# Where VectorE reads a plain key, multiplies by the cosine and forms weight sums in an attention layer

## The chip, the cores and the metric

The kernel runs on one core of one Trainium2 chip. A core has five engines that run at the same time, each through its own queue in order: TensorE (PE, matrix products; PEld is its weight load), VectorE (DVE), ScalarE (ACT), GpSimd (POOL) and SyncE (SP), whose queue issues the DMA loads here. They wait for each other through semaphores. PE, DVE and ACT reach the accumulators in PSUM; everything else lies in SBUF.

The metric is the device time of one execution in microseconds (us), the median over repeated runs. A profile is one further execution, recorded instruction by instruction; its span runs from the first to the last instruction of the program.

## The reference

The model is a trunk of two layers on one sequence of 512 positions and width 1024, in float32: a dilated attention mixer, a gated ConvFFN, a Mamba-2 mixer, another ConvFFN, a final norm. The change lies in the attention mixer alone. There are 8 heads of width 128 and three groups of queries, keys and values, with dilations 1, 4 and 16:

```
qkv = (h @ w_qkv).reshape(bsz, s, N_ATTN_GROUPS, 3, ATTN_HEADS_PER_GROUP, ATTN_HEAD_DIM)
q = apply_partial_rope(qkv[:, :, :, 0], cos, sin)
k = apply_partial_rope(qkv[:, :, :, 1], cos, sin)
...
o_g, lse_g = dilated_window_attention(q[:, :, g], k[:, :, g], v[:, :, g], dil, ATTN_WINDOWS[g] // dil)
```

`apply_partial_rope` turns the first 32 of a head's 128 rows: each is multiplied by a cosine, and its partner row, multiplied by a sine, is added. The results of the three groups are mixed by a softmax over their log sums, and a product with `w_o` and the residual follow.

## The kernel before

Weights come as float32 and are split into a high and a low part (`hi` by ACT, `lo` by a DVE subtraction of two SBUF operands, L127 and L128, or L328 and L331); each block of a product is three PE matmuls (`mm3`, L138). The normalised input lies in SBUF, split in the same way (`xh`, `xl`).

A head needs seven projections: a query and a key in each of three groups, and the value `v0` of group 0 (groups 1 and 2 have theirs from a separate step). They are made in two ways:

- Plain: `ready` loads and splits the weights, `qk_products` makes 24 matmuls into a PSUM bank, and `qk_read` (L460) reads it: DVE multiplies by the cosine table `cr` out of PSUM (L464), DVE swaps the 32 rows with their partners (`stream_shuffle`, L467), POOL multiplies them by the sine table (L468) and adds them to the tile (L469). Group 0 is always plain.
- As a `Pair` (L475), query and key of group 1 or 2 together, with seven products of half size in place of eight: `load_sevens` (L302) issues four loads; `sums()` forms four sums of weights on DVE, each of 512 columns (L317, L318, L320, L321; L318 reads what L317 wrote, L320 what L318 wrote); `split("ab")`, `split("cd")` split the four weights; `block(i)` makes 12 matmuls; `query` and `key` add the products up out of PSUM on DVE and end in a shuffle and POOL's sine product (`swap`, L537); `turn` (L543) makes the cosine multiplication on DVE (L546) and the sum of the 32 rows on POOL (L547).

`v0_step` makes the product of `v0`; DVE scales it into the tile `tv` (L554); `v0_turn` has PE transpose it (L561, tile `pv`).

`attend(h)` is a generator with the steps of one head's attention: scores of four blocks of 128 queries (`scores(0)`, `scores(2)`: PE L659 to L661, then DVE masks and takes maxima, L665 and L669), exponentials on ACT, the shares of the groups (`join`), transposes of the probabilities (L714), products with the values (L722, L727), and the head's output `o` (ACT L759, DVE L760). The scores of a head read its plain key after L469.

`attend_and_project(h)` (L813) runs head h's attention between the projections of head m = h + 1, for h = 0 to 5. It holds two pairs: `one`, group 1 of head m, loaded and split by the head before, and `two`, group 2, loaded and split here. After them come the plain query and key of group 0 and `v0`. `next_pair(m + 1)` (L572), the generator `follow`, prepares the next head's `one`: its first step makes the pair's loads and its four sums, the second splits a and b, the third c and d. (For the last head, whose projections are all plain, it loads two plain weights in place of that.) For h = 3 the steps in `after` stand in its place. Before the first head, L591 to L634 do the same for head 0, and `following` prepares head 1.

Order: inside `tc.manual_schedule(engines=WRITTEN)` PE, DVE and ACT take their instructions in the order in which the program text makes them. POOL and SP are ordered by a planner that simulates the program. Buffers come from small rings: four of 1024 columns for raw weights, two for the fourth raw weight, two for the shuffled rows; a load waits until the user of its buffer is done.

Of the kernel before, what the change touches and what calls it, by code (L numbers as in the profile page):

```python
# [53 lines left out]
def trunk(ctx: ExitStack, tc: tile.TileContext, A, out):  # L54
# [23 lines left out]
    def t2(name, tag, bufs, pool=k2, dtype=F32):  # L78
        return pool.tile([P, 512], dtype, tag=tag, name=name, bufs=bufs)
# [69 lines left out]
    def project(src, name, low=V, cut=None):  # L149

        if name in early:
            return early.pop(name)
        if name in begun:
            t, hi, lo, at = begun.pop(name)
        else:
            hi, lo = loaded.pop(name) if name in loaded else load_unit(src, name, low=low)
            t, at = mm_bank(name), 0
        for k in range(at, KD):
            if cut and cut[0] == k:
                cut[1]()  # L160
            mm3(t, hi, lo, k, xh[k], xl[k], k == 0, k == KD - 1)
        return t
# [233 lines left out]
    def combine(j):  # L396

        x1, x2 = xps[2 * j], xps[2 * j + 1]
        w1, w2, m1 = col(C_MIX + 2 * j), col(C_MIX + 2 * j + 1), minus[:, 2 * j : 2 * j + 1]
        (ah, al), (bh, bl) = high_low(f"ta{j}"), high_low(f"tb{j}")  # L400
        d, t = (t2(f"{n}{j}", "pr", 7, s3) for n in ("d", "t"))
        e, t4 = d[:, H1], d[:, H0]
        V.tensor_tensor(d[:, H0], x1[:, H1], x1[:, H0], op=ALU.subtract)
        SC.activation(e, x2[:, H1], AF.Copy, scale=w2)
        SC.activation(ah[:, H0], d[:, H0], AF.Copy, scale=w1)
        V.scalar_tensor_tensor(
            al[:, H0], d[:, H0], w1, ah[:, H0].bitcast(F32), op0=ALU.mult, op1=ALU.subtract
        )
        V.scalar_tensor_tensor(t[:, H0], d[:, H0], m1, e, op0=ALU.mult, op1=ALU.add)
        V.scalar_tensor_tensor(t[:, H1], x1[:, H1], m1, e, op0=ALU.mult, op1=ALU.add)  # L410
        V.scalar_tensor_tensor(t4, x2[:, H0], w2, t[:, H0], op0=ALU.mult, op1=ALU.subtract)
        for h, l, at, src in ((ah, al, H1, t[:, H0]), (bh, bl, H0, t[:, H1]), (bh, bl, H1, t4)):
            SC.copy(h[:, at], src)
            V.tensor_tensor(l[:, at], src, h[:, at].bitcast(F32), op=ALU.subtract)
        combined.append(((ah, al), (bh, bl)))
# [31 lines left out]
    def name_of(h, g, c):  # L447
        return f"qk{h}{g}{c}"

    def ready(h, g, c):  # L450
        u = A["wqk"][h * 7 + 2 * g + c]
        loaded[name_of(h, g, c)] = load_unit(u, name_of(h, g, c))

    def ready_v0(h):
        loaded[f"v0{h}"] = load_unit(A["wqk"][h * 7 + 6], f"v0{h}")

    def qk_products(h, g, c, cut=None):
        return project(A["wqk"][h * 7 + 2 * g + c], name_of(h, g, c), cut=cut)

    def qk_read(h, g, c, p):  # L460
        n = name_of(h, g, c)
        t = t2(n, "qk", 10, s3)
        at, of = (in_blocks, by_residue) if g == 0 else ((lambda ap: ap),) * 2
        V.tensor_tensor(at(t), of(p), of(cr), op=ALU.mult)  # L464
        rot = t2("rot" + n, "rot", 2, s3)
        R = slice(0, ROPE)
        V.stream_shuffle(rot[R, :], p[R, :], SWAP)  # L467
        G.tensor_tensor(rot[R, :], rot[R, :], sr[R, :], op=ALU.mult)  # L468
        G.tensor_tensor(at(t)[R], at(t)[R], of(rot)[R], op=ALU.add)  # L469
        qk[h, g, c] = t  # L470
# [4 lines left out]
    class Pair:  # L475
# [53 lines left out]
        def key(self):  # L529
            k = self.out[1]  # L530
            V.tensor_tensor(k[:, H0], self.s[0], self.r[2], op=ALU.add)
            V.tensor_tensor(k[:, H1], k[:, H0], self.s[1], op=ALU.add)
            V.tensor_tensor(k[:, H0], k[:, H0], self.r[3], op=ALU.add)
            self.swap(1)
            self.turn(1)

        def swap(self, c):  # L537
            R = slice(0, ROPE)
# [11 lines left out]
    def v0_step(h):  # L550
        n = f"v0{h}"
        p = project(A["wqk"][h * 7 + 6], n)
        t = t2("t" + n, "vt", 1, s3)
        V.tensor_tensor(in_blocks(t), by_residue(p), by_residue(rbc), op=ALU.mult)  # L554
        v0[h] = t

    def v0_turn(h):
        t = v0[h]
        pv = aux_bank("pv")
        for j in range(4):  # L560
            T.transpose(pv[:, j * P : (j + 1) * P], t[:, j * P : (j + 1) * P], ident)  # L561
        v0[h] = t2(f"v0{h}", "v0", 2, s3)
        SC.copy(v0[h], pv)
# [8 lines left out]
    def next_pair(h):  # L572

        if h == NH - 1:
            ready(h, 0, 0)
            yield
            ready(h, 0, 1)
            yield
        else:
            pair = begun_pair[h] = Pair(h, 1)  # L580
            pair.sums()
            yield
            pair.split("ab")
            yield
            pair.split("cd")
        yield
# [4 lines left out]
    with tc.manual_schedule(engines=WRITTEN):  # L591
        load2(1)
        V.tensor_tensor(cr, cr, rbc, op=ALU.mult)
        second[0]()
        combine(1)
        load2(2)
        V.tensor_tensor(sr[0:ROPE, :], sr[0:ROPE, :], rbc[0:ROPE, :], op=ALU.mult)
        second[1]()
        combine(2)
        load2(3)  # L600
        second[2]()
        combine(3)
        ready(0, 0, 0)
        one = Pair(0, 1)
        second[3]()
        one.sums()
        one.split("ab")
        p = qk_products(0, 0, 0)
        qk_read(0, 0, 0, p)
        one.split("cd")  # L610
        ready(0, 2, 0)
        for i in range(3):
            one.block(i)
        one.query(0)
        for i in range(3, 6):
            one.block(i)
        one.query(1)
        ready(0, 2, 1)
        one.block(6)
        one.turn(0)  # L620
        one.key()
        p = qk_products(0, 2, 0)
        ready(0, 0, 1)
        qk_read(0, 2, 0, p)
        p = qk_products(0, 2, 1)
        ready_v0(0)
        qk_read(0, 2, 1, p)
        p = qk_products(0, 0, 1)
        qk_read(0, 0, 1, p)
        following = next_pair(1)  # L630
        next(following)
        next(following)
        v0_step(0)
        next(following)  # L634
# [178 lines left out]
    def attend_and_project(h, after=()):  # L813

        core, m = attend(h), h + 1
        follow = next_pair(m + 1)
        with tc.manual_schedule(engines=WRITTEN):
            one, two = begun_pair.pop(m), Pair(m, 2)
            next(core)
            next(core)  # L820
            v0_turn(h)
            two.sums()
            one.block(0)
            one.block(1)
            two.split("a")
            one.block(2)
            one.query(0)
            two.split("b")
            for i in range(3, 6):
                one.block(i)  # L830
            one.query(1)
            one.block(6)
            one.turn(0)
            one.key()
            next(core)
            two.split("c")
            two.block(0)
            two.block(1)
            next(core)
            two.block(2)  # L840
            two.query(0)
            two.split("d")
            ready(m, 0, 0)
            for i in range(3, 6):
                two.block(i)
            two.query(1)
            ready(m, 0, 1)
            next(core)
            two.turn(0)
            next(core)  # L850
            next(core)
            two.block(6)
            two.key()
            p = qk_products(m, 0, 0)
            qk_read(m, 0, 0, p)
            ready_v0(m)
            if not after:
                next(follow)
            p = qk_products(m, 0, 1, cut=(6, lambda: next(core)))
            next(core)  # L860
            qk_read(m, 0, 1, p)
            for f in after[:2] or (lambda: next(follow),) * 2:
                f()
            v0_step(m)
            next(core, None)
            for f in after[2:]:
                f()
# [950 lines left out]
```

## Time and profile before

| | |
|---|---|
| median of three runs | 1627.27 us (1624.9 to 1629.9) |
| the profiled execution | 1625.19 us |
| its span | 1623.4 us |
| mean granted TensorE clock | 0.996 |
| PE busy | 1599.6 us, 99% of the span |
| DVE, ACT, POOL busy | 1247.5, 787.7 and 579.7 us |

A row of the timeline gives start and duration in us, engine, line, operation, the tile written and those read, shape and count, and in brackets the time for which the engine was idle before it and what ended that. Consecutive instructions with the same tiles are one row, and rows overlap a little, because an engine starts an instruction before the one ahead has drained. A row of the waits gives the total, the number and the longest. A row of the windows gives a stretch, its length, each engine's busy time (and instructions), the granted clock of TensorE, and the DMA load. Attention with its projections takes the span's first 490 us.

### The profile page before, as it was taken

The page shows a single profiled execution, that of the slowest core. Times are in us where ns is not written, and L with a number is a line of the kernel's source. Part 1 is how long each engine was busy: PE and PEld are TensorE (multiplying, and loading weights), DVE is VectorE, ACT ScalarE, POOL GpSimd, SP SyncE. Part 2 cuts the span into 40 slices and gives each one's busy share as a digit, 9 for nine tenths or more (in the row PEclk, how much of TensorE's full clock was granted, in tenths as well). Part 3 has the DMA queues.
Part 4 walks back from the last instruction along what each step waited for, and adds up shares of the span by engine and source line. Part 5 has one row for each costly group of instructions (what it writes and reads, how often), then busy time and mean ns, then how long its engine had stood idle before and what let it go on. Part 6 is the DMA issues. An engine that isn't in the chain of part 4 may idle for free.

```text
span 1623.4 us, 24013 instructions
## 1 busy us (share of the span) xinstructions
PE 1599.6 (99%) x9080; PEld 1408.0 (87%) x9080; DVE 1247.5 (77%) x1949; ACT 787.7 (49%) x1362; POOL 579.7 (36%) x432
## 2 busy tenths in 40 slices
PE   9999999999999999999999999999999999999998
PEld 8888889898888889989988888888888888988987
DVE  7798887388556778868857889988898687876864
ACT  5355455265564544444445455544453454444443
POOL 0434444044432554653321222220122275365230
PEclk9999999999999999999999999999999999999999
DMA  6322223223334323423423333243332322342341
GB/s 220 92 85 88 82 72 111 72 79 98 98 117 148 112 66 97 151 60 96 140 82 119 120 118 115 92 127 127 127 115 78 101 84 76 102 133 79 93 129 52
DMA packets 63331, 168.48 MB, mean 104 GB/s; under 512 B 7344, under 2 KB 10800, under 8 KB 63216
## 3 DMA queue, kind: packets, MB, share of 16 engines
q1 hardware_dynamic: 62656, 166.42, 32.6%
q8 instruction: 71, 1.16, 0.3%
q10 hardware_dynamic: 560, 0.53, 0.1%
q14 instruction: 44, 0.36, 0.1%
HBM read 163.19 MB, written 3.74 MB: 103 GB/s over the span
## 4 chain that ended last, share of the span: by engine, by line
PE 87%; DVE 7%; ACT 3%; POOL 2%; issue 1%; DVEq 0%; POOLq 0%; ACTq 0%
PE u L136 29%; PE v L136 6%; PE z L136 5%; PE wso L136 5%; PE xs L136 5%; PE qk L136 5%; PE b L136 3%; PE c L136 3%; PE wo L136 2%; PE wd L136 2%; PE wz L136 2%; POOL rotqk L468 1%; ACT oth L686 1%; ACT pr L707 1%; PE py L1391 1%
## 5 line engine op out<-in xcount | busy, mean ns | idle before, releaser
L136 PE MATMUL u<-xh,hi_u 128*128 128x512 f32 x704 | 269.4, 383 | 0.0
L136 PE MATMUL u<-xh,lo_u 128*128 128x512 f32 x704 | 269.0, 382 | 0.0
L136 PE MATMUL u<-xl,hi_u 128*128 128x512 f32 x704 | 266.6, 379 | 0.0
L128 DVE TENSOR_TENSOR lo_u<-raw_u,hi_u 128x1024 fp32r<-128x1024 f32 x88 | 123.8, 1416 | 39.8 <-ACT hi_u L127 39.8
L136 PEld LDWEIGHTS u<-xh,lo_u 128*128 128x128 f32 x704 | 131.7, 187 | 24.5
L136 PEld LDWEIGHTS u<-xl,hi_u 128*128 128x128 f32 x704 | 131.7, 187 | 23.9
L136 PEld LDWEIGHTS u<-xh,hi_u 128*128 128x128 f32 x704 | 131.7, 187 | 22.2 <-issue 0.4
L127 ACT CAST hi_u<-raw_u 128x1024 fp32r<-128x1024 f32 x88 | 91.8, 1048 | 106.7 <-PE u L136 61.3
L960 DVE SCALAR_TENSOR_TENSOR au<-u,par,au 128x511 f32<-128x511 f32 (+1 forms) x152 | 113.4, 746 | 20.4 <-ACT au L958 18.0
L541 POOL TENSOR_TENSOR rotqk<-rotqk,sr 32x512 f32<-32x512 f32 x26 | 53.2, 2047 | 184.6 <-DVE rotqk L540 184.6
L985 POOL TENSOR_TENSOR au<-au,au 128x512 f32<-128x512 f32 x43 | 58.0, 1348 | 169.0 <-DVE au L960 155.2
L1336 POOL TENSOR_TENSOR xdd<-xdt,dec 128x384 f32<-128x384 f32 x16 | 18.0, 1139 | 240.3 <-DVE xdt L1335 240.3
L973 DVE TENSOR_TENSOR u<-u,rbc 128x512 f32<-128x512 f32 x76 | 52.9, 696 | 63.8 <-PE u L136 63.4
L468 POOL TENSOR_TENSOR rotqk<-rotqk,sr 32x512 f32<-32x512 f32 x22 | 51.2, 2327 | 71.2 <-DVE rotqk L467 71.2
L958 ACT ACTIVATE au<-u,par 128x512 f32<-128x512 f32 x76 | 59.1, 778 | 24.1 <-DVE u L973 22.5
L136 PE MATMUL qk<-xh,hi_qk 128*128 128x512 f32 x176 | 68.3, 388 | 0.0
L136 PE MATMUL qk<-xh,lo_qk 128*128 128x512 f32 x176 | 67.5, 384 | 0.0
L136 PE MATMUL qk<-xl,hi_qk 128*128 128x512 f32 x176 | 66.9, 380 | 0.0
L1136 POOL TENSOR_TENSOR xr<-xr,sums 128x512 f32<-128x512 f32 x16 | 33.1, 2067 | 82.6 <-DVE sums L1134 82.6
L239 POOL TENSOR_TENSOR ssum<-ssum,sq 128x512 f32<-128x512 f32 x21 | 32.5, 1547 | 83.7 <-ACT sq L238 83.3
L1445 POOL TENSOR_TENSOR lm<-lm,cb 128x512 f32<-128x512 f32 x32 | 47.5, 1508 | 25.5 <-ACT lm L1378 25.5
L982 ACT ACTIVATE au<-au 128x512 f32<-128x512 f32 x44 | 27.8, 631 | 54.9 <-DVE au L960 54.9
(3988 smaller groups left out, 5089.7 us busy)
## 6 DMA issues: line engine op xcount, KB each, us to landing
raw_u<-in_wup SPq DMA_DIRECT2D x88, 512.0 KB, 3.5
raw_qk<-in_wqk SPq DMA_DIRECT2D x22, 512.0 KB, 3.4
raw_xs<-in_win SPq DMA_DIRECT2D x16, 512.0 KB, 3.8
raw_z<-in_win SPq DMA_DIRECT2D x16, 512.0 KB, 3.5
lm<-rows SPq DMA_DIRECT2D x32, 256.0 KB, 5.3
raw_wso<-in_wso SPq DMA_DIRECT2D x16, 512.0 KB, 3.4
raw_v<-in_wv SPq DMA_DIRECT2D x12, 512.0 KB, 4.1
raw_wd<-in_wdn SPq DMA_DIRECT2D x16, 384.0 KB, 3.3
```

The lines of the kernel that those rows point to most:

```text
L127: SC.copy(hi[:, s], raw[:, s])
L128: low.tensor_tensor(lo[:, s], raw[:, s], hi.bitcast(F32)[:, s], op=ALU.subtract)
L136: T.matmul(in_turns(dst), w, in_turns(x), start=first, stop=last, skip_group_check=skip)
L239: add.tensor_tensor(ssum, ssum, sq, op=ALU.add)
L468: G.tensor_tensor(rot[R, :], rot[R, :], sr[R, :], op=ALU.mult)
L541: G.tensor_tensor(rot[R, :], rot[R, :], sr[R, :], op=ALU.mult)
L958: latest["tap"] = SC.activation(dst, src, AF.Identity, bias=col(c_b), scale=col(c_w + taps - 1))
L960: V.scalar_tensor_tensor(dst[:, j:], src[:, : S - j], col(c_w + taps - 1 - j), dst[:, j:], op0=ALU.mult, op1=ALU.add,)
L973: V.tensor_tensor(dst, p, rbc, op=ALU.mult)
L985: by.tensor_tensor(ab[1], ab[0], ab[1], op=ALU.mult)
L1136: G.tensor_tensor(low3, low3, v.unsqueeze(1).to_broadcast([P, 2, 256]), op=ALU.add)
L1445: G.tensor_tensor(t, t, cb, op=ALU.mult)
```

## The change

Three parts, all in the order in which the text makes instructions; no computation is added or removed.

- `key()` no longer ends in `turn(1)`; each of its three callers calls it. Two call it straight behind `key()`. In `attend_and_project` the `turn(1)` of `one` stands behind the second scores' masks and maxima and behind `two.split("c")`.
- In `attend_and_project` with no `after`, the first step of `follow` (the next pair's loads and sums) stands behind the read of the plain key of group 0 and no longer ahead of its product.
- Before the first head, the first step of `following` stands ahead of the product of head 0's plain key, no longer behind its read.

```
@@ class Pair, key()
             V.tensor_tensor(k[:, H0], k[:, H0], self.r[3], op=ALU.add)
             self.swap(1)
-            self.turn(1)
@@ before the first head
         one.turn(0)
         one.key()
+        one.turn(1)
         p = qk_products(0, 2, 0)
...
         qk_read(0, 2, 1, p)
+        following = next_pair(1)
+        next(following)
         p = qk_products(0, 0, 1)
         qk_read(0, 0, 1, p)
-        following = next_pair(1)
-        next(following)
         next(following)
         v0_step(0)
         next(following)
@@ attend_and_project
             one.key()
             next(core)
             two.split("c")
+            one.turn(1)
             two.block(0)
...
             two.block(6)
             two.key()
+            two.turn(1)
             p = qk_products(m, 0, 0)
             qk_read(m, 0, 0, p)
             ready_v0(m)
-            if not after:
-                next(follow)
             p = qk_products(m, 0, 1, cut=(6, lambda: next(core)))
             next(core)
             qk_read(m, 0, 1, p)
-            for f in after[:2] or (lambda: next(follow),) * 2:
+            for f in after[:2] or (lambda: next(follow),) * 3:
                 f()
             v0_step(m)
```

More of the change, by code (lines that the diff above doesn't have):

```diff
@@ L534, in key @@
             self.swap(1)
-            self.turn(1)
         def swap(self, c):
@@ L621, in trunk @@
         one.key()
+        one.turn(1)
         p = qk_products(0, 2, 0)
@@ L627, in trunk @@
         qk_read(0, 2, 1, p)
+        following = next_pair(1)
+        next(following)
         p = qk_products(0, 0, 1)
         qk_read(0, 0, 1, p)
-        following = next_pair(1)
-        next(following)
         next(following)
@@ L836, in attend_and_project @@
             two.split("c")
+            one.turn(1)
             two.block(0)
@@ L853, in attend_and_project @@
             two.key()
+            two.turn(1)
             p = qk_products(m, 0, 0)
@@ L856, in attend_and_project @@
             ready_v0(m)
-            if not after:
-                next(follow)
             p = qk_products(m, 0, 1, cut=(6, lambda: next(core)))
@@ L861, in attend_and_project @@
             qk_read(m, 0, 1, p)
-            for f in after[:2] or (lambda: next(follow),) * 2:
+            for f in after[:2] or (lambda: next(follow),) * 3:
                 f()
```

## The prediction

> **What bounds the kernel now.** I read the page first, then PE's waits from 50 to 480 us, then the timelines of PE, DVE and POOL around the longest of them, then the windows for the clock.
>
> ```profile
> span 1623.4 us, 24013 instructions
> PE 1599.6 (99%) x9080; PEld 1408.0 (87%) x9080; DVE 1247.5 (77%) x1949; ACT 787.7 (49%) x1362; POOL 579.7 (36%) x432
> ```
>
> ```profile
> PE sc L659 <- POOL qk L469: 11.8, 4, 3.0
> PE pv L561 <- DVE tv L554: 2.1, 1, 2.1
> PE qk42r L136 <- DVE loc_qk L331: 0.4, 1, 0.4
> ...
> PE qk52r L136 <- DVE loc_qk L331: 0.3, 1, 0.3
> ```
>
> PE sets the end; what the change can save is PE's idle time and what follows from it. Scores waited four times, some 3 us each, for the plain key that POOL finishes late. Once the transposes of `v0` waited for DVE, and in six heads one weight product waited 0.35 us for a split. The page itself counts 24 us without a busy PE. Here is the first long wait, on POOL, DVE and PE.
>
> ```profile
> 122.00 1.26 POOL L547 TENSOR_TENSOR qk<-qk,rotqk 32x512 f32<-32x512 f32 x1
> 123.23 2.24 POOL L468 TENSOR_TENSOR rotqk<-rotqk,sr 32x512 f32<-32x512 f32 x1
> 125.55 1.61 POOL L469 TENSOR_TENSOR qk<-qk,rotqk 32x512 f32<-32x512 f32 x1
> 130.38 4.43 POOL L468 TENSOR_TENSOR rotqk<-rotqk,sr 32x512 f32<-32x512 f32 x1 [3.22 <-DVE rotqk L467]
> 134.89 1.60 POOL L469 TENSOR_TENSOR qk<-qk,rotqk 32x512 f32<-32x512 f32 x1
> ```
>
> ```profile
> 122.13 2.22 DVE L128 TENSOR_TENSOR lo_v<-raw_v,hi_v 128x1024 fp32r<-128x1024 f32 x1
> 124.27 1.75 DVE L317 TENSOR_TENSOR rawa_qk<-q_qk,rawb_qk 128x512 f32<-128x512 f32 x1
> 126.06 1.66 DVE L318 TENSOR_TENSOR rawb_qk<-rawa_qk 128x512 f32<-128x512 f32 x1
> 127.75 0.69 DVE L320 TENSOR_TENSOR rawc_qk<-rawc_qk,rawb_qk 128x512 f32<-128x512 f32 x1
> ...
> 128.96 0.68 DVE L464 TENSOR_TENSOR qk<-qk,cr 128x512 f32<-128x512 f32 x1
> 129.57 0.73 DVE L467 STREAM_SHUFFLE rotqk<-qk 32x512 f32<-32x512 f32 x1
> 130.21 1.20 DVE L331 TENSOR_TENSOR loa_qk<-rawa_qk,hia_qk 128x1024 fp32r<-128x1024 f32 x1
> ...
> 133.61 1.75 DVE L331 TENSOR_TENSOR lod_qk<-q_qk,hid_qk 128x512 fp32r<-128x512 f32 x1
> 135.29 0.67 DVE L554 TENSOR_TENSOR tv<-v,rbc 128x512 f32<-128x512 f32 x1
> 135.89 1.07 DVE L760 TENSOR_TENSOR o<-o,po 128x512 f32<-128x512 f32 x1
> ```
>
> ```profile
> 132.90 0.61 PE L727 MATMUL pg<-pt,v 128*128 128x128 f32 x4
> 136.54 0.80 PE L659 MATMUL sc<-qk,qk 128*128 128x128 f32 x2 [3.04 <-POOL qk L469]
> ...
> 373.47 0.49 PE L659 MATMUL sc<-qk,qk 128*128 128x128 f32 x2 [2.93 <-POOL qk L469]
> ...
> 375.12 0.60 PE L561 MATMUL pv<-ident,tv 128*128 128x128 f32 x4
> ```
>
> The key is read at 128.96, behind four sums; its POOL part then takes 130.38 to 136.49, while PE stands still from 133.51. DVE works without a gap from 122.13 to 136.96. DVE instructions with two SBUF operands and POOL's exclude each other: L318 takes 1.66 where L320 takes 0.69, while POOL's L469 runs; and POOL's L468 lasts 4.43 while DVE's splits follow each other, until `lod` gives way (1.75). Neither the read out of PSUM (0.68) nor the shuffle (0.73) suffers. Alone, such a POOL instruction takes 1.26 (L547).
>
> ```profile
> 136.50:140.00 3.50, 3.46 (x16) 3.28 (x17) 1.41 (x7) 0.89 (x4) 0.00 (x0) 0.55 0.50 170
> 186.00:191.00 5.00, 4.96 (x27) 4.91 (x28) 3.98 (x14) 2.56 (x9) 0.00 (x0) 0.66 0.34 111
> 235.60:239.00 3.40, 3.37 (x15) 3.19 (x16) 1.34 (x7) 0.80 (x4) 0.00 (x0) 0.56 0.53 180
> 373.40:377.00 3.60, 3.53 (x29) 3.48 (x30) 2.89 (x13) 1.66 (x7) 0.01 (x1) 1.00 0.27 102
> ```
>
> These windows follow the four waits. PE is busy in all of them, but after three the granted clock is 0.55, 0.66 and 0.56. So a wait costs more than its idle time: 3.5 x 0.45 + 5.0 x 0.34 + 3.4 x 0.44 = 1.6 + 1.7 + 1.5 = 4.8 us.
>
> The Trainium skill's page "TensorE: Matmul & The Clock Gate" (Part 1) has the clock fall to half after an idle window of about 3.4 us, in windows that run freely. The idle times here are below that, and three of four still lost clock; the measurement decides. By the rule to the letter there would be no loss, and the sum below would be 4.8 us smaller; three windows in four speak against that, so it gets no chance of its own.
>
> **The plain key ahead of the sums (in the step of h = 0, 1, 2 and 4, which ends in the scores of heads 1, 2, 3 and 5).** Without the sums in front, DVE reads the key where `lo_v` ends, 124.27, and has shuffled at 125.6. POOL is then in the query's two instructions: L468 runs beside read and shuffle, to 125.5, L469 to 126.8. L317 now meets L469 and ends at 127.4. L318 must wait for L317's result; POOL takes that gap (as the first sums did against POOL above) for the key's L468, to 128.6; L318 ends at 129.2; POOL's L469 follows to 130.5, L320 ends at 131.0, L321 at 131.6. The key is ready at 130.5, PE wants it at 133.5: the 11.8 us go, and the 4.8 of clock. Their cover is 3 us.
>
> What is late next is `tv`. Behind L321 stand `loa`, `lob`, `loc` (1.2 each, starts 1.13 apart: to 135.0), `lod`, now without POOL, 0.69 (135.6), `tv` (136.2). Contested instructions of DVE are `lo_v` and three sums, before `lo_v`, two sums and `lod`; so `tv` ends 0.25 later than its 135.96. PE starts scores at 133.5 and needs 1.65 for them at full clock (373.47 to 375.12), so it wants `tv` at 135.1: a new wait of 1.1 a head, 4.4 in all. Bounds: one contested instruction less, 0.1; one or two more, at 1.05 each (1.75 less 0.69, and a little overlap), 2.2 to 3.2. I take 1.1, since each POOL instruction can hold DVE up once.
>
> The moved step issues four loads as well. Each goes out when its buffer comes free, and no other load stands between the old place and the new one, so SP's queue keeps its order. For h = 5 the step is a plain load and split; the waits above show none of PE's there, and the split moves behind a read that then comes earlier: nothing.
>
> **The first pair's sums ahead of head 0's key.**
>
> ```profile
> 76.52 0.74 DVE L467 STREAM_SHUFFLE rotqk<-qk 32x512 f32<-32x512 f32 x1
> 81.18 0.69 DVE L464 TENSOR_TENSOR qk<-qk,cr 128x512 f32<-128x512 f32 x1 [3.92 <-PE qk L136]
> ...
> 91.63 0.28 DVE L665 CUSTOM_DVE_ANT_0 pr<-sc,mask 128x128 f32<-128x128 f32 x1
> ```
>
> ```profile
> 84.32 1.62 POOL L469 TENSOR_TENSOR qk<-qk,rotqk 32x512 f32<-32x512 f32 x1
> ```
>
> ```profile
> 86.26 0.38 PE L659 MATMUL sc<-qk,qk 128*128 128x128 f32 x2
> ...
> 90.03 0.55 PE L561 MATMUL pv<-ident,tv 128*128 128x128 f32 x3 [2.06 <-DVE tv L554]
> ```
>
> ```profile
> 72.60 0.33 SPq L313 DMA_DIRECT2D rawc_qk<-in_wqs  x1
> ```
>
> ```profile
> rawc_qk<-in_wqs SPq DMA_DIRECT2D x1, 256.0 KB, 2.9
> ```
>
> The last load lands at 75.5, before the shuffle ends at 77.26. DVE was idle for 3.92; the sums need 4.8 with two of them contested, as from 124.27 to 129.04, or 2.8 with none. So the key is read at 82.0, and its POOL part starts at 83.4 beside `loa` and `lob`, the order in which it was starved at 130.38. `lob` ends at 85.6, DVE then waits for `v0`; POOL ends at 86.9 and 88.2. Head 0's scores, which found their key at 85.94 and started at 86.26, now wait 2.0, and the transposes, which had waited 2.06, no longer do: gain 0.1, up to 2.1 if POOL gets in at once. I take 0.1, by the 4.43 row.
>
> Head 0 also tells what DVE's new lag costs elsewhere. Behind `tv` DVE has `o` (1.07) and then the masks of the scores, which so start some 1.0 after PE's transposes. Head 0 started them 1.6 after (91.63 against 90.03) and lost no more at its splits than the other heads. So the lag costs nothing beyond the wait for `tv`.
>
> The Trainium skill, "SBUF — State Buffer" (Who interferes with whom), says that of two contenders the one that issues first gets the pair of ports for its whole instruction. By that POOL would come right behind `loa`, and head 0 would gain 1.1 more; the 4.43 row, in which two further splits went ahead, speaks against it.
>
> **The cosine behind the split.**
>
> ```profile
> 103.91 0.69 DVE L546 TENSOR_TENSOR qk<-qk,cr 128x512 f32<-128x512 f32 x1
> ...
> 107.05 1.21 DVE L331 TENSOR_TENSOR loc_qk<-rawc_qk,hic_qk 128x1024 fp32r<-128x1024 f32 x1
> ```
>
> ```profile
> 108.32 0.38 PE L136 MATMUL qk12r<-xh,loc_qk 128*128 128x256 f32 x1 [0.36 <-DVE loc_qk L331]
> ```
>
> L546 leaves the stretch ahead of `loc`, which ends 0.6 sooner; the wait of 0.36 goes in six heads, 2.2 us. Now it stands behind `loc`, ahead of a query sum and `lod`. POOL's L547 of this key moves with it and may hold `lod` up for 1.26. PE needs `lod` only in block 6, behind the 24 matmuls of blocks 4 and 5, which use `loc`: these are its cover. Without it six heads would lose 1.26 less 0.36 each, 5.4 us. I take the 2.2; the bounds are 2.2 and -5.4.
>
> **Sum.** 11.8 + 4.8 - 4.4 + 0.1 + 2.2 = 14.5 us. Against the profiled execution, 1625.19 (span 1623.4), that is 1610.7. The three runs' median, 1627.27, lies 2.1 higher. I put a part of that down to how many of the four waits lose clock, which then no longer counts, and add 1.3: 1612. On this scale no change is 1626.5.
>
> **Rivals.** First, `tv` in time and head 0 gaining its 2.1: 11.8 + 4.8 + 2.2 + 2.1 = 20.9, so 1606. For it: a split that stands in a gap of POOL's costs DVE nothing. Against it: DVE has no gap of its own before `tv`, and its instructions there alone last to 135.
>
> Second, that the change doesn't do what it says: the key's POOL part is starved by sums and splits until `lod`, as it was from 130.38 on, and scores wait as before. Then only 2.2 and 0.1 are left: 1624. For it: the 4.43. Against it: head 0's old order was what the other heads get now, and its key was ready 4.8 after the read began (81.18 to 85.94).
>
> Third, slower: DVE becomes the bound at `pv`. A head gains (11.8 + 4.8) / 4 = 4.15 less its wait for `tv`. If all four sums and all four splits had to let a POOL instruction by, that is four more at 1.05, the wait would be 1.1 + 4.2 = 5.3, long enough to cost the clock again as the waits of 3 us did (4.8). The balance is 4 x (4.15 - 5.3) + 2.3 - 4.8 = -7.1, so 1634; it decides from a wait of 3.5. For it: DVE is without a gap for 15 us there. Against it: only five POOL instructions fall in the stretch, and four of them already count.
>
> **How the numbers follow.** Forecast 0.64, its own range 1608 (wait for `tv` 0.05) to 1620 (3.2); first rival 0.12, second 0.13, third 0.06; 0.05 I leave to POOL's and SP's planned order coming out differently elsewhere, either way. 0.3% of 1627, some 5 us, is about what a measurement of this kernel tells from no change. Below 1622.4 lie forecast, first rival and some of the rest, 0.79; within, the second, 0.14; slower, the third, 0.07. The range runs from the first rival, 1606, to 1623, short of the second.
>
> **What would show it.** Right: no wait of scores for L469 from head 1 on; full clock at 136, 187 and 235 us; a wait of `pv` for `tv` near 1.1 in four heads; one of head 0's scores near 2; no wait for `loc`. Wrong: an L468 over 4 us for a key of heads 1, 2, 3 or 5; a wait for `tv` above 3; new waits of PE beyond 490 us.

## The result, and the profile after

The changed kernel takes 1609.46 us (1608.42 to 1609.78) where the kernel before takes 1626.09 in the same comparison. The ratio is 0.9893, 95% interval 0.9874 to 0.9912: some 17 us less, 1.1%. The profiled execution took 1609.21 us against 1625.19. Of the runs below, one execution of the variant with four added matmuls, of 4830 us, is left out of its range.

The first two lines of the page of the changed kernel, and PE's waits from 50 to 480 us (total, number, longest):

```profile
span 1607.4 us, 24012 instructions
...
PE 1593.4 (99%) x9080; PEld 1403.4 (87%) x9080; DVE 1253.2 (78%) x1949; ACT 786.8 (49%) x1362; POOL 568.4 (35%) x432
```

```profile
PE pv L560 <- DVE tv L553: 4.6, 4, 1.2
PE sc L659 <- POOL qk L469: 1.6, 1, 1.6
PE pp L714 <- ACT pr L707: 0.2, 1, 0.2
```

One source line fell away, so L560 is the former L561, L553 the former L554. The four waits of scores for the plain key are gone. In their place stand four waits of the transposes for `tv`, and head 0's scores now wait once, 1.6 us. The six waits for `loc` are gone. PE's waits in this stretch fell from 16.1 to 6.4 us; the 0.2 for `pp` among them is not new, since before it falls just past 480 us, so 9.8 us are saved. The windows behind the four places, with the granted clock in the third column from the end, show the second half of the gain:

```profile
135.00:140.00 5.00, 4.59 (x40) 4.59 (x41) 4.86 (x16) 2.83 (x11) 0.00 (x0) 1.00 0.63 230
180.90:186.00 5.10, 5.01 (x44) 5.01 (x45) 4.96 (x16) 3.23 (x12) 0.00 (x0) 1.00 0.63 215
226.50:231.00 4.50, 4.42 (x39) 4.42 (x40) 4.36 (x15) 2.65 (x11) 0.00 (x0) 1.00 0.68 242
359.80:365.00 5.20, 5.13 (x45) 5.14 (x46) 5.06 (x16) 3.37 (x12) 0.00 (x0) 1.00 0.43 161
```

All four read 1.00; before, three of them had read 0.55, 0.66 and 0.56. The 4.8 us of clock are back. Here is the first of these places on POOL, DVE and PE, to be laid beside the stretch from 122 us before:

```profile
122.70 2.25 POOL L468 TENSOR_TENSOR rotqk<-rotqk,sr 32x512 f32<-32x512 f32 x1
125.02 1.77 POOL L469 TENSOR_TENSOR qk<-qk,rotqk 32x512 f32<-32x512 f32 x1
126.76 1.73 POOL L468 TENSOR_TENSOR rotqk<-rotqk,sr 32x512 f32<-32x512 f32 x1
128.57 1.62 POOL L469 TENSOR_TENSOR qk<-qk,rotqk 32x512 f32<-32x512 f32 x1
```

```profile
123.74 0.68 DVE L464 TENSOR_TENSOR qk<-qk,cr 128x512 f32<-128x512 f32 x1
...
124.98 0.66 DVE L317 TENSOR_TENSOR rawa_qk<-q_qk,rawb_qk 128x512 f32<-128x512 f32 x1
125.68 1.67 DVE L318 TENSOR_TENSOR rawb_qk<-rawa_qk 128x512 f32<-128x512 f32 x1
127.38 1.66 DVE L320 TENSOR_TENSOR rawc_qk<-rawc_qk,rawb_qk 128x512 f32<-128x512 f32 x1
128.96 1.78 DVE L321 TENSOR_TENSOR q_qk<-rawa_qk,q_qk 128x512 f32<-128x512 f32 x1
130.66 1.21 DVE L331 TENSOR_TENSOR loa_qk<-rawa_qk,hia_qk 128x1024 fp32r<-128x1024 f32 x1
...
134.07 0.68 DVE L331 TENSOR_TENSOR lod_qk<-q_qk,hid_qk 128x512 fp32r<-128x512 f32 x1
134.67 0.68 DVE L553 TENSOR_TENSOR tv<-v,rbc 128x512 f32<-128x512 f32 x1
```

```profile
132.47 0.39 PE L659 MATMUL sc<-qk,qk 128*128 128x128 f32 x2
...
135.41 0.66 PE L560 MATMUL pv<-ident,tv 128*128 128x128 f32 x4 [1.23 <-DVE tv L553]
```

The key's two POOL instructions end at 130.2, more than 2 us before PE's scores at 132.5. Three of the four sums are held up by POOL (1.67, 1.66, 1.78 against 0.66 alone), `lod` no longer is, and `tv` ends at 135.35, 1.2 after PE wants it. In head 0 the key's first POOL instruction meets the splits:

```profile
83.50 3.30 POOL L468 TENSOR_TENSOR rotqk<-rotqk,sr 32x512 f32<-32x512 f32 x1 [2.50 <-DVE rotqk L467]
86.88 1.25 POOL L469 TENSOR_TENSOR qk<-qk,rotqk 32x512 f32<-32x512 f32 x1
```

Past 400 us the two traces run side by side, 15.9 to 16.1 us apart: nothing was given back later, and nothing more was gained.

### The profile page after: what moved, and what is told of

It reads as the page before. It is cut to its first block, busy times and chain, and to the rows that moved or that the text cites. A ratio compares the mean times of both kernels' runs of the same rounds, so it can differ in the third digit from the quotient of the medians.

```text
span 1607.4 us, 24012 instructions
## 1 busy us (share of the span) xinstructions
PE 1593.4 (99%) x9080; PEld 1403.4 (87%) x9080; DVE 1253.2 (78%) x1949; ACT 786.8 (49%) x1362; POOL 568.4 (35%) x432
## 4 chain that ended last, share of the span: by engine, by line
PE 90%; DVE 5%; ACT 3%; issue 1%; POOL 0%; POOLq 0%; DVEq 0%; ACTq 0%
PE u L136 29%; PE v L136 6%; PE z L136 5%; PE wso L136 5%; PE xs L136 5%; PE qk L136 4%; PE b L136 3%; PE c L136 3%; PE wo L136 2%; PE wd L136 2%; PE wz L136 2%; ACT oth L686 1%; ACT pr L707 1%; PE py L1391 1%; PE pf L1399 1%; PE pst L1346 1%
## 5 line engine op out<-in xcount | busy, mean ns | idle before, releaser
L540 POOL TENSOR_TENSOR rotqk<-rotqk,sr 32x512 f32<-32x512 f32 x26 | 50.2, 1930 | 176.9 <-DVE rotqk L539 176.9
L468 POOL TENSOR_TENSOR rotqk<-rotqk,sr 32x512 f32<-32x512 f32 x22 | 42.6, 1934 | 58.0 <-DVE rotqk L467 58.0
```

## The experiments

Three kernels make one part of the change each; the others ask what a wait costs, what holds `tv` up, and what the order could still give. Times are medians, with the range of the executions and the ratio to the kernel before.

**The cosine alone.**

```
             self.swap(1)
-            self.turn(1)
...
             two.split("c")
+            one.turn(1)
```

> The kernel before with one part of the change: the cosine multiplication of the first pair's key behind the split of c, nothing else. Theory (that split bounds PE in six heads): the six waits of 0.36 us for loc go; the four waits of scores near 3 us and the half clock behind them stay. The idle time saved is 2.2 us; from the start of one matmul to the next such a wait cost 0.64 in place of 0.11 (107.68 to 108.32), so 6 x 0.53 = 3.1 us: 1623.0 against 1626.1. Rival (VectorE's order alone sets when the plain key is read, whatever PE does): the waits of scores grow by what is saved, and the time moves by less than 1 us.

Measured: 1625.49 (1621.57 to 1628.93) against 1625.65, ratio 0.9996 (0.9985 to 1.0007). PE's waits:

```profile
PE sc L659 <- POOL qk L469: 13.7, 4, 3.5
PE pv L560 <- DVE tv L553: 2.1, 1, 2.1
```

The rival was right. No wait for `loc` is left, but the four waits of scores grew from 11.8 to 13.7 us: PE came earlier, and the key came when DVE and POOL let it. My theory took the saving for PE's alone. By itself, this part is worth nothing that can be measured.

**The plain key alone.**

```
-            if not after:
-                next(follow)
...
-            for f in after[:2] or (lambda: next(follow),) * 2:
+            for f in after[:2] or (lambda: next(follow),) * 3:
```

> The kernel before with one part of the change: the plain key read ahead of the next pair's sums in heads 1, 2, 3 and 5, nothing else. Theory: the four waits of scores go and with them the half clock; waits of the value's transposes for tv of 1.1 to 1.2 us come in their place; the six waits for loc stay at 0.36, since the lag of VectorE is caught up before the second pair, as head 0 of the kernel before showed. 16.6 less 3.1 for the cosine and 0.4 for head 0: 1613.0. Rival: the lag of 2.4 us which VectorE now has behind PE's transposes is carried to the split of c: waits for loc of over 1 us in four heads, 1616 or more.

Measured: 1612.38 (1611.94 to 1612.67), ratio 0.9916 (0.9902 to 0.9931).

```profile
PE pv L561 <- DVE tv L554: 5.5, 5, 2.0
PE qk42r L136 <- DVE loc_qk L331: 0.3, 1, 0.3
...
PE qk52r L136 <- DVE loc_qk L331: 0.3, 1, 0.3
```

This part carries the change: 13 of the 17 us. The waits for `loc` are 0.31 to 0.33, no longer than before, so DVE's lag was caught up and the rival fell. Of the 5.5 us, head 0 has 2.04 and the other four heads some 0.87 each, where the whole change has 1.06 to 1.23. So a part of what the cosine saves at `loc` comes back at `tv`, 0.3 in each of four heads; the rest of it stays.

**Head 0's sums alone.**

```
+        following = next_pair(1)
+        next(following)
         p = qk_products(0, 0, 1)
         qk_read(0, 0, 1, p)
-        following = next_pair(1)
-        next(following)
```

> The kernel before with one part of the change: the first pair's sums ahead of head 0's plain key, nothing else. Theory: the wait of the transposes for tv (2.06 us) goes and one of head 0's scores for the key (1.6 us) takes its place, because GpSimd cannot get between two splits: 0.4 us less, 1625.7, no change that a measurement tells. Rival: GpSimd gets in behind the first split and all 2.1 us are gained: 1624.0.

Measured: 1625.18 (1619.47 to 1627.94), ratio 0.9992 (0.9979 to 1.0004). The wait of 2.06 for `tv` became one of 1.60 for the key, as the theory had it. The three parts alone give 0.2, 13.3 and 0.5 us, of which only the 13.3 is clear of noise, 14.0 together, and the whole gives 16.6. The cosine pays once the key no longer bounds the scores: in the profiles the changed kernel is 1.28 us ahead of the key alone at head 1's transposes (135.41 against 136.69), 2.45 at head 5's and 2.9 behind the layer, with full clock in both, so 1.7 of it is the cosine's. The rest lies further ahead, where the key alone also ran at half clock from 89.80 to 93.21 us, behind its wait of 2.04 in head 0. This kernel's profile also held a surprise. Its four waits of 3 us lost no clock at all:

```profile
135.30:140.30 5.00, 4.98 (x41) 4.93 (x42) 4.26 (x15) 2.82 (x10) 0.00 (x0) 1.00 0.30 104
183.40:188.40 5.00, 5.00 (x42) 4.95 (x43) 4.28 (x15) 2.82 (x10) 0.00 (x0) 1.00 0.33 109
231.50:236.50 5.00, 5.00 (x41) 4.95 (x42) 4.28 (x15) 2.82 (x10) 0.00 (x0) 1.00 0.33 117
367.90:372.90 5.00, 5.00 (x42) 4.95 (x43) 4.28 (x15) 2.82 (x10) 0.00 (x0) 1.00 0.14 53
```

That execution took 1619.5, the median 1625.2. In the cosine's profile, with waits of 3.3 to 3.5, all four lost it. So the same wait may or may not cost the clock.

The kept traces show what decides. A stretch at half clock in the layer lasts 3.41 us (one lasted two of these), and within a profile these stretches begin whole multiples of 3.41 us apart, so the clock changes on a grid. Here are two steps of that grid at a wait of 3.04 us of the kernel before, then two at a wait of 3.01 us of this kernel:

```profile
132.79:136.21 3.42, 0.72 (x7) 0.52 (x5) 3.42 (x4) 1.07 (x1) 3.34 (x2) 1.00 0.90 245
136.21:139.62 3.41, 3.08 (x12) 2.90 (x13) 1.56 (x6) 0.51 (x3) 0.28 (x1) 0.50 0.58 198
```

```profile
229.64:233.05 3.41, 1.55 (x12) 1.50 (x13) 2.86 (x7) 0.00 (x0) 1.73 (x2) 1.00 0.81 256
233.05:236.46 3.41, 3.41 (x32) 3.41 (x31) 3.24 (x12) 2.82 (x10) 0.00 (x0) 1.00 0.20 75
```

In the first, 2.70 us of the wait lie in one step (3.42 less 0.72 busy), and the next step has half clock. In the second the wait is shared by two steps, with at most 1.87 us in one (edges not rounded), and the clock stays. In the thirteen profiles, up to 1595 us, PE was idle for 2.04 to 3.29 us of the step ahead of each of the ten falls, and for no more than 1.87 us of any other step at full clock. So what decides is how a wait lies on the grid, and that differs from execution to execution.

**The wait filled with matmuls.** Nothing of the change; PE works through the wait.

```
                 sc = side_bank("sc")
+                if i == 0 and h in (1, 2, 3, 5):
+                    for _ in range(12):
+                        T.matmul(sc, xh[0][:, 0:P], xh[0], start=True, stop=True)
```

> The kernel before, no part of the change; ahead of the first scores of heads 1, 2, 3 and 5 PE makes twelve matmuls of 512 columns on the layer's input into the bank that the scores then overwrite (0.22 us each, 2.7 us, less than the wait of 3). Theory (the half clock comes from PE's idle time): the waits of scores shrink to some 0.4 us, the granted clock behind them is 1.00 in all heads, and the time falls by the clock's share alone, 4.8 us: 1621.3. Rival (the half clock belongs to the scores and transposes themselves, with their small matmuls): the clock falls to half behind three or four of them again, and the time stays at 1626.

Measured: 1622.00 (1620.85 to 1622.80), ratio 0.9973 (0.9963 to 0.9982). The four waits are 1.0 us in all, and the clock behind them is full:

```profile
137.20:142.20 5.00, 4.92 (x41) 4.87 (x42) 4.26 (x15) 2.82 (x10) 0.03 (x1) 1.00 0.33 115
185.40:190.40 5.00, 5.00 (x42) 4.95 (x43) 4.23 (x15) 2.82 (x10) 0.00 (x0) 1.00 0.30 108
233.50:238.50 5.00, 4.97 (x42) 4.92 (x43) 4.24 (x15) 2.82 (x10) 0.00 (x0) 1.00 0.33 111
369.90:374.90 5.00, 4.97 (x42) 4.92 (x43) 4.24 (x15) 2.82 (x10) 0.00 (x0) 1.00 0.17 57
```

The key comes no sooner, the work of the kernel is the same with 48 matmuls added, and it is 3.7 us faster: this is the share of the clock behind these four waits, between the medians of 29 and 11 executions. The small matmuls of the scores are not the cause of the half clock, PE's standing still is. The spread shrinks from 7.7 us (1623.1 to 1630.8 before) to 2.0. In the same profile the wait of 2.06 in head 0, not filled, was followed by a window at 0.66:

```profile
89.00:94.00 5.00, 4.78 (x28) 4.78 (x29) 4.86 (x16) 2.31 (x9) 0.00 (x0) 0.66 0.72 233
```

**Eight and four of them.** The same kernel with `range(8)` and with `range(4)`.

> The kernel before with eight filling matmuls of 512 columns ahead of the first scores of heads 1, 2, 3 and 5 in place of twelve: the waits of scores there are some 1.25 us. Theory (idle stretches of up to 1.7 us have lost no clock in any profile here, those of 2.05 us in three of four, those of 3 us and more in seven of twelve): full clock behind all four waits, and the time of the twelve, 1622.0. Rival (any wait of PE for the key costs clock in proportion to its length): 1622.0 plus 1.2/3.0 of 3.65, 1623.5.

> The kernel before with four filling matmuls there: waits of some 2.15 us. Theory: such waits lose clock in some heads and not in others, by how they fall on windows of 3.4 us that run on by themselves; the time spreads over more than 4 us and its median lies between 1622.0 and 1625.7. Rival (a threshold of 3 us): full clock, 1622.0 with the small spread of the twelve (2 us).

Measured with eight, waits of 1.13 to 1.21: 1621.56 (1620.95 to 1622.13), ratio 0.9972 (0.9960 to 0.9983). With four, waits of 1.98 to 2.09: 1623.82 (1620.74 to 1626.61), ratio 0.9986 (0.9975 to 0.9996). With a wait of 1.2 in place of 0.2 to 0.3 the time is no longer and no clock is lost: the key comes when it did. At 2.1 the executions spread over 6 us, from the fast end of the eight to the median of the kernel before and a little past it: both theories for these two held, both rivals fell. In the profile that was taken with four, all four windows are at 1.00: its waits have at most 1.84 us in one step of the grid. The spread of the times tells that other executions lost clock.

**The plain query without POOL's part.** In heads 1, 2, 3 and 5.

```
-        G.tensor_tensor(rot[R, :], rot[R, :], sr[R, :], op=ALU.mult)
-        G.tensor_tensor(at(t)[R], at(t)[R], of(rot)[R], op=ALU.add)
+        if not (h in (1, 2, 3, 5) and g == 0 and c == 0):
+            G.tensor_tensor(rot[R, :], rot[R, :], sr[R, :], op=ALU.mult)
+            G.tensor_tensor(at(t)[R], at(t)[R], of(rot)[R], op=ALU.add)
```

> The changed kernel without GpSimd's two instructions on the plain query of heads 1, 2, 3 and 5: its sine part is left out, so that part of the rotation is not computed. Theory (tv is late because GpSimd's instructions hold the sums up, 1.05 us each): two instructions fewer in the stretch, tv ends 1.0 to 2.0 us sooner, the transposes wait 0 to 0.2 us in place of 1.2: 1605. Rival (VectorE's own work between the read of the key and tv is too long): the waits stay at 1.1 to 1.2 us, 1609.5.

Measured: 1604.65 (1604.57 to 1605.56), against 1609.35 (1609.20 to 1610.32) for the changed kernel beside it.

```profile
126.71 1.66 DVE L320 TENSOR_TENSOR rawc_qk<-rawc_qk,rawb_qk 128x512 f32<-128x512 f32 x1
128.29 0.68 DVE L321 TENSOR_TENSOR q_qk<-rawa_qk,q_qk 128x512 f32<-128x512 f32 x1
...
132.90 0.68 DVE L554 TENSOR_TENSOR tv<-v,rbc 128x512 f32<-128x512 f32 x1
```

L321 takes 0.68 in place of 1.78, and the waits for `tv` fall to 0.13 and less. Two POOL instructions fewer hold up one sum fewer, 1.1 us, and that was the whole wait. So POOL's work on DVE's is enough to make `tv` late. That DVE's own length plays no part is not shown: the next variant takes 1.7 us of DVE's own work from ahead of `tv`, and the waits go as well.

The expectation for the changed kernel run again was:

> The changed kernel itself, beside the variants of the same call. Waits of the value's transposes for tv of 1.1 to 1.2 us in heads 1, 2, 3 and 5, 1.6 us of head 0's scores for its key, full clock throughout: 1609.5, with a spread of its runs of under 2 us, where the kernel before spreads over 5, since how many of its waits lose the clock differs from run to run.

It held: the waits for `tv` are 1.04 to 1.21, and the ratio is 0.9901 (0.9885 to 0.9917). One further wait of 0.9 us of the last head's scores came up in its profile, and that was its slowest execution, 1610.32.

**The value's scaling ahead of two splits.**

```
-            for f in after[:2] or (lambda: next(follow),) * 3:
+            for f in after[:2] or (lambda: next(follow),) * 2:
                 f()
             v0_step(m)
+            if not after:
+                next(follow)
```

> The changed kernel with the step that splits c and d of the next pair behind the scaling of the value (tv) and no longer ahead of it, in heads 1, 2, 3 and 5. Theory (what delays tv is only what stands ahead of it on VectorE): tv ends 1.9 us sooner, the four waits of the transposes (4.65 us idle, and 0.17 each of matmul overlap) go, and the splits of c and d, wanted two products later, cost nothing, as in head 0: 1604.2. Rival (VectorE's whole work up to the scores' masks is the bound): a wait of like size comes back at the splits of the next pair or at loc, and the time stays within 1 us of 1609.5.

Measured: 1605.32 (1604.84 to 1605.48), ratio 0.9874 (0.9858 to 0.9890), 4.0 less than the changed kernel. The four waits are gone, and two short ones (0.06 and 0.14) came for `loc` and for a copy of ACT's. The theory holds, 1.1 us short of its sum; where that went I did not follow up.

**The same in head 0.** There `v0_step(0)` stands ahead of both splits as well.

> As value_early, and in head 0 the scaling of the value stands ahead of both splits of the first pair. Theory: VectorE then waits for the value's product behind the key's shuffle, GpSimd gets its two instructions in without the splits (3.3 us become 1.3), and the wait of head 0's scores, 1.6 us, goes; the first block's weights come 0.1 to 0.4 us late: 1602.7. Rival: the late splits make PE wait at the first block for what was gained, or scores wait as before: 1604.2.

Measured: 1604.97 (1604.61 to 1605.47), ratio 0.9873 (0.9857 to 0.9889), 0.35 less than with the order of head 0 unchanged; the two ranges overlap.

```profile
83.19 1.27 POOL L468 TENSOR_TENSOR rotqk<-rotqk,sr 32x512 f32<-32x512 f32 x1 [2.51 <-DVE rotqk L467]
84.54 1.28 POOL L469 TENSOR_TENSOR qk<-qk,rotqk 32x512 f32<-32x512 f32 x1
```

```profile
94.55 0.38 PE L136 MATMUL qk11r<-xh,hic_qk 128*128 128x256 f32 x1 [0.81 <-ACT keptqk L517]
```

Without splits beside it L468 takes 1.27 in place of 3.30, and the wait of scores is gone. Half of that comes back at the fifth block: the splits now put the masks off, ACT's queue has the exponentials ahead of its copy, and PE waits 0.81 for that. Theory and rival each had one half.

**The splits of c and d behind the masks.** The step that was last in a head now runs in the next one.

```
+            if not after:
+                rest.append(lambda: next(follow))
...
             next(core)
+            if rest:
+                rest.pop()()
             next(core)
```

> The variant with both early values, and the step that splits c and d moved once more, behind the masks of the next head's first scores, in every head. Theory: what was left there was ScalarE late with the kept products because the masks, and so the exponentials ahead of them in its queue, came behind both splits (0.8 us in the first head, 0.14 in another); it goes: 1604.0. Rival: the splits of c and d, now behind the masks, come too late for the fifth block and PE waits for them as long: 1605.0 or more.

Measured: 1602.73 (1602.38 to 1603.26), ratio 0.9856 (0.9842 to 0.9870). All that PE still waits for between 50 and 460 us is this:

```profile
PE qk11r L136 <- DVE qk L524: 0.2, 1, 0.2
```

It is 1.3 us better than the theory said, for a reason that no run here shows, and 6.6 below the changed kernel: the best version here. PE's waits in this stretch are gone; whether another order of PE's own matmuls would be shorter was not tried.

## Why the prediction was right

The forecast was 1612 and the result 1609.46, inside the forecast's own range. The mechanism was the one foreseen, and most terms came out by themselves.

- **The key ahead of the sums, 11.8 and 4.8.** Right. The sc waits are gone, and the clock is full at the places named. I had said 130.5 minus 124.27, 6.2 us, from the read of the key to its end on POOL; it is 6.45 (123.74 to 130.19). The filling matmuls show the 4.8 to be a property of that execution: between medians the clock behind these four waits is worth 3.7. The prediction put nothing on the clock behind head 0's wait of 2.06 for `tv`. It lost none in the profile before, but in three of the six profiles that have this wait, and then the way from the transposes to the wait for `loc` took 1.5 us longer (89.22 to 109.02 in the kernel with twelve matmuls, 90.03 to 108.32 in the kernel before). The changed kernel waits 1.62 there, and lost none.
- **`tv` 1.1 late, 4.4 in all.** Right: 1.23, 1.18, 1.06 and 1.18, 4.65 in all. I had three of the sums held up as L317, L318 and L320; it was L318, L320 and L321. The number of three was right, which of them was not.
- **Head 0, 0.1.** Its scores wait 1.62 where I said 2.0, so 0.4. POOL got in behind `lob`, as the 4.43 row had it; by the rule in the Trainium skill's page "SBUF — State Buffer" (Who interferes with whom), that who issues first goes first, it would have gone behind `loa`, and the trace does not agree. Its L468 lasted 3.30, which is `loa` and `lob` and its own time.
- **DVE's lag costs nothing.** Right, by the key alone: waits for `loc` as before.
- **The cosine, 2.2.** The waits for `loc` went as forecast, but I let the saving pass straight to the end, and that step was wrong. The kernel with this part alone shows that DVE and POOL, not PE, set the time of the scores there, and with the key moved a third of a microsecond in four heads still comes back at `tv`. From head 1 on this part is worth 1.7 beside the key.
- **A term that I left out** made up for that, which was luck. A wait costs PE more than its idle time, because matmuls no longer overlap. Of the kernel before:

```profile
107.68 0.27 PE L136 MATMUL qk12r<-xl,hic_qk 128*128 128x256 f32 x1
108.32 0.38 PE L136 MATMUL qk12r<-xh,loc_qk 128*128 128x256 f32 x1 [0.36 <-DVE loc_qk L331]
```

  From start to start this is 0.64, where undisturbed neighbours are 0.11 apart: 0.53 lost at an idle time of 0.36. Eleven waits became five (without `pp`); if each costs these 0.17 us beside its idle time, six of them are 1.0 us, an estimate. Idle time 9.8, clock 4.8 and this 1.0 are 15.6 of the 16.0 us between the two profiled executions.
- **The 1.3 added to the sum.** Wrong, and half of the miss of 2.5: the sum itself gave 1610.7. I had put the median of three, 1627.27, partly down to executions that lose more clock. The reason holds (the spread is the clock's, and the changed kernel has nearly none), but such a loss goes with the change and must not be added to what remains.

Of the rivals, a starved key did not come about: POOL got in between the sums. That it does so because each sum waits for the one before, as the prediction argued, is not shown: its L469 at 128.57 went ahead of L321, which does not read what L320 wrote. And DVE as the bound at `pv` came in the small size that the forecast already held.

## What to carry to other kernels

Where PE is 99% busy, the few microseconds in which it stands still can still be the whole gain, and each costs its idle time, the lost overlap of its matmuls, and, where it leaves PE idle for some 2 us within one step of the clock's grid, half the clock for 3.41 us. Look then for the last producer, not the last instruction: here it was POOL, kept waiting by DVE instructions with two SBUF operands, and the cure was to let it run beside reads out of PSUM, a shuffle and the sums, not beside a row of splits. Two savings on one path do not add up before the one that bounds it is gone, so price the second one against the state after the first.

## What the runs showed of the hardware

The clock's fall after a wait of PE is settled by how the wait lies on a grid of 3.41 us: in these profiles the clock fell behind each step in which PE was idle for 2.04 us or more, and behind none with 1.87 or less. From one execution to the next that looks like chance, at waits well below the 3.4 us that the Trainium skill gives for an idle window in "TensorE: Matmul & The Clock Gate" (Part 1). That the windows run freely, as the page has it, agrees with the traces; a wholly idle window as the condition does not. Waits of 1.2 us lost no clock in any profile here and the times agree within 1.2 us; with waits of 2.1 the executions spread over 5.9 us; at 3.0 three of four lost it in one profile and none of four in another. Nearly the whole spread of the kernel before, 7.7 us, is this, as the fillers show. Of its 29 executions beside the first variants, the eight with a mean granted clock of 0.997 took 1623.1 to 1623.5, and the two with 0.991 and 0.992 took 1630.4 and 1630.8.

Between DVE and POOL, a POOL instruction waited through the split that was running and one more that was issued after it (3.30 us), or two more (4.43 us). It got in between sums: ahead of L318 and L320, of which each reads the one before, and ahead of L321, which does not. Why it gets in ahead of some independent instructions and not of others is not settled by these runs.
